# ScalarE and GpSimd in the order of the source in the recurrence and the attention of a hybrid decoder layer, and the work on loaded data issued later than the load

## The chip, the cores and the metric

The kernel runs on one core of one Trainium2 chip. Its engines are TensorE (PE in the profile: matmuls and transposes), VectorE (DVE), ScalarE (ACT), GpSimd (POOL) and the queue of SyncE (SP) that issues the DMAs. The metric is the device time of one launch in microseconds (us), lower is better.

## The reference

One decoder layer, 1024 tokens by 1024 features, all in float32:

```python
u = rmsnorm(x, mix_pre_norm)
z = u @ w_in                       # q,k,v of 3 groups x 4 heads; r,k,v and LoRA inputs of 8 RWKV heads; gates
# (A) dilated sliding-window attention, (window, dilation) = (128,1), (512,4), (2048,16)
q, k = rope(q), rope(k)
s = where(valid, q . k[t - dil*j] / 8, -inf);  o_g = softmax(s) @ v;  lse_g = m + log(den)
o_attn = sum_g softmax_g(lse)[g] * o_g
# (B) RWKV-7, per head, state 64 x 64, over the 1024 tokens
z = z + (token_shift(z) - z) * mu
decay = exp(-exp(-softplus(-(w0 + tanh(xw) @ w2)) - 0.5));  a = sigmoid(a0 + xa @ a2);  g = sigmoid(xg) @ g2
state = state * w_t + (state @ a_t) b_t^T + v_t k_t^T;  y_t = state @ r_t
o_rwkv = (groupnorm(y) * ln_w + ln_b + sum(r*k*r_k) * v) * g
# merge, MLP, per-layer embedding
h = x + rmsnorm((gate_a * (o_attn @ w_attn_up) + gate_b * (o_rwkv @ w_rwkv_up)) @ w_out)
h = h + rmsnorm(square(relu(rmsnorm(h) @ w_ff_in)) @ w_ff_out)
h = h + rmsnorm((p @ w_ple) * sigmoid(h @ w_ple_gate))
```

## The kernel before

**Arithmetic.** A float32 product is made of three passes: each operand is split into a high part (`uh`, `wh`) and a low part (`ul`, `wl`), and `mm3` sums high x high, high x low and low x high into one PSUM bank. So a weight tile of 128 x 1024 that SP has loaded as `wr` (`wload`) is split before it is used: ACT copies it to `wh`, POOL subtracts for `wl`. The pool of these three names has two buffers each. A dense body is a projection of one such tile with all tokens in two halves `z` of 512, with an evacuation behind each half (`add_z`, `zhalf`).

**Stages.** Norm and transposition of the input (0 to 44 us of the profiled span); recurrence (to about 540) in four pairs of heads w = 0 to 3, worked in 16 chunks of 64 tokens as a chain of small matmuls: `elementwise` (decay `En`, `Ep`, key `kk`, `BK`), `invert` and `fold` (the matrices `TM`, `AR` of a chunk), `scan` (over the chunks: PE's `q`, then DVE adds into `AR`), `read_out` (`y`), `post` (the group norm: ACT evacuates `y` to `yc`, squares it, PE sums (`hv`), ACT takes the root `vc`, spreads it to `rb`, PE transposes it (`yt`), three DVE operations on `yc`, and SP stores `oscr<-yc`; there is one `yc` tile, and `post` runs twice per pair, b = 0 and 1). Then the attention (to about 815) in six units n = 0 to 5 (three groups, two pairs of heads each): scores `sc`, masked by DVE into `SB`, exponent on ACT, transposes `pt`, DVE copies them to `PB`, and `po` is the product with the values. `q` and `k` of a unit are evacuated by `qk`: two ACT copies into the tile `qk`, four DMAs that exchange its halves into `sw`, DVE's product with the cosines in place (`qk<-qk,rope`), POOL's product of `sw` with the sines, DVE's sum. `combine` joins the groups (to 832); then merge, out projection, MLP (1040 to 1690) and the embedding.

**What sets the order.** PE's instructions stand in the order of the source for the whole kernel. That order is made by a planner at build time, `Order` (`sch`): chains are generators that say when they can go on by the planner's own clock (`sch.t`), and while none is due, `fill` issues the next matmuls of a dense body. `Engine` (V, S, G) adds up planned costs of DVE, ACT and POOL, `Loads` a planned 2.5 us (`HOP_DMA`) for each DMA. DVE stands in the order of the source only from the start of the recurrence to the start of `attention` (`in_turn`). Everything else, ACT, POOL and SP throughout and DVE in the other stages, is ordered by the framework's scheduler, which places an instruction by its own estimate of when its inputs are there.

All DVE, ACT and POOL operations are issued by one helper, line L108, and all DMAs by L121; PE's lines are `mm` L244, `tr` L252, and `mm3` L261, L263, L265. In after.py they are L115, L128, L267, L275 and L284, L286, L288.

Of the kernel before, what the change touches and what calls it, by code (L numbers as in the profile page):

```python
# [57 lines left out]

class Written:
# [17 lines left out]
class Engine:  # L77
# [3 lines left out]
    def __init__(self, eng, order, fixed, per):  # L81
        self.eng, self.order, self.fixed, self.per = eng, order, fixed, per
        self.end, self.table = 0.0, None
        self.spare = None

    def __getattr__(self, name):
        f = getattr(self.eng, name)

        def call(*a, **kw):
            n = max(math.prod(x.shape[1:]) for x in a if hasattr(x, "shape"))  # L90
            o = self.order
            us = self.fixed + n * self.per * (1.8 if name == "transpose" else 1.0)
            if name == "activation" and a[2] in TABLE and self.table != TABLE[a[2]]:
                us += 1.3
                self.table = TABLE[a[2]]
            ins = [x for x in (*a[1:], *kw.values()) if hasattr(x, "shape")]
            ready = max((o.written.since(x, self) for x in ins), default=0.0)
            while self.spare and self.end + SPARE < ready:
                spare, self.spare = self.spare, None
                dep, t = o.dep, o.t  # L100
                self.spare = spare if next(spare, None) else None
                o.dep, o.t = dep, t
            self.end = max(self.end, o.t, ready) + us
            for x in (a[0], kw.get("accum_out")):
                if x is not None:
                    o.written.put(x, self.end, self)
            o.dep = max(self.end, o.dep)
            return f(*a, **kw)  # L108
        return call
# [14 lines left out]
class Order:  # L124
# [4 lines left out]
    def __init__(self):  # L129
        self.t = self.dep = 0.0  # L130
        self.chains = []
        self.dense = []
# [20 lines left out]

    def pick(self):
# [10 lines left out]
    def fill(self):  # L165
        if self.cur is None:
            self.cur, self.nxt = self.nxt or self.pick(), None
            if self.cur is None:
                return False
            if not self.cur[1]:  # L170
                self.ahead()
# [43 lines left out]
def layer(ctx: ExitStack, tc: tile.TileContext, x, pT, wz, wup, w_out, wff1, w_ff2, w_ple, w_pleg,  # L215
# [5 lines left out]
    V = Engine(nc.vector, sch, 0.18, 0.00104)  # L221
# [60 lines left out]
    def wload(src, n=1024):  # L282
# [3 lines left out]
        S.activation(hi[:, :n], raw[:, :n], AF.Copy)  # L286
        lo = wpool.tile([128, 1024], F32R, name="wl")
        G.tensor_tensor(lo[:, :n], raw[:, :n], hi[:, :n], OP.subtract)  # L288
# [260 lines left out]
    def elementwise(w):  # L549
# [7 lines left out]
        yield from wait(lambda: "r" in RKV[w] and "k" in RKV[w])  # L557
# [232 lines left out]
    def read_out(w):  # L790
        d = U[w]
        AR, TM, UV = d["AR"], d["TM"], d["UV"]
        for b in range(2):
# [12 lines left out]
            sch.busy[tag] = sch.dep + 1.5  # L806
# [3 lines left out]
    def post(w, b, ps, tag):  # L810
        pc = lambda c: pr[:, c + w:c + w + 1]
        ts = halves[b]
        og = rtile([128, 512], "og", "pg")
# [51 lines left out]
    A = {}  # L865
# [8 lines left out]
    def add_attn(n):  # L874
# [10 lines left out]

        def qk(x):
            def evac(h, ps):
# [7 lines left out]
                if h == 1:  # L895
# [4 lines left out]
                    G.tensor_tensor(sw, sw, rope_t[g][:, 1], OP.mult)  # L900
                    V.tensor_tensor(z, z, sw, OP.add)
                    A[n]["qk"] = sch.dep
# [14 lines left out]
    def attention():  # L917
        yield from wait(lambda: ("P", NU - 1, 1) in done)
        in_turn.__exit__(None, None, None)
# [28 lines left out]
        for n in range(6):  # L948
# [6 lines left out]
            yield sch.until(A[n]["qk"])  # L955
# [8 lines left out]
        yield from combine(OT, OTB[:, 1], stat)  # L964
# [103 lines left out]
    def combine(OT, OA, stat):  # L1068
        sraw = rtile([128, 768], "sraw", "v")
        SY.dma_start(sraw, cst[:, C_SEL:C_SEL + 768])  # L1070
        sel = rtile([128, 6, 128], "sel", "px", F32R)
        V.tensor_copy(sel.rearrange("p a b -> p (a b)"), sraw)
# [32 lines left out]
        for b in range(2):  # L1105
# [18 lines left out]
            OA_t.append(sch.dep)  # L1124

# [3 lines left out]
    in_turn = tc.manual_schedule(engines={mybir.EngineType.DVE})  # L1129
# [32 lines left out]
    def load_or(w, eng):  # L1162
# [3 lines left out]
        S.activation(hl[:, 0], raw, AF.Copy)  # L1166
        eng.tensor_tensor(hl[:, 1], raw, hl[:, 0], OP.subtract)
        orT[w] = (hl[:, 0], hl[:, 1])

    def merge(j):  # L1170
        def load():
# [6 lines left out]
            for n in range(2):  # L1178
                SY.dma_start(gt[n], g_scr[2 * j + n])
                S.activation(gt[n], gt[n], AF.Sigmoid)  # L1180
# [537 lines left out]
```

## Time and profile before

| | |
|---|---|
| median of 3 runs | 1836.97 us (1831.67 to 1838.75) |
| profiled execution | 1831.63 us, span 1829.7 us |
| mean granted PE clock | 0.984 |
| busy: PE, DVE, ACT, POOL | 97%, 57%, 40%, 42% of the span |

The rows of the profile name the engine, the line, the operation and out<-in by the names of tiles. "[3.77 <-ACT wh]" behind a row is the time that the engine stood idle before it, and the instruction that ended that; in the table of waits the three numbers are microseconds in all, how often, and the longest. A matmul's own end is modelled, so PE's idle time is read from the waits and not from the gaps between rows.

### The profile page before, as it was taken

To read this page: it belongs to the slowest core of one execution; us is meant where nothing else is said; L and a number is where in the kernel's file an instruction comes from. 1 tells how busy PE (TensorE), PEld (TensorE's weight loads), DVE (VectorE), ACT (ScalarE), POOL (GpSimd) and SP (SyncE) were. 2 spreads that over 40 slices of the span, in tenths; PEclk is the share of its full clock that TensorE was granted. 3 is DMA by queue.
4 is the path that set the end of the run, shared out by engine and by line. 5 is a ranking of instruction groups with operands and counts; after the bars stand their busy time and mean duration, and the time that the engine had idled before them with its cause. 6 is when DMAs were issued, how large, how long until landed. Compare 5 with 4: busy or idle time off the path is not lost.

```text
span 1829.7 us, 25894 instructions
## 1 busy us (share of the span) xinstructions
PE 1769.9 (97%) x10192; PEld 1436.4 (79%) x10192; DVE 1044.6 (57%) x1866; ACT 725.5 (40%) x1300; POOL 775.1 (42%) x507
## 2 busy tenths in 40 slices
PE   9998989999989999999999999999999999999898
PEld 8887767777877777777888788888888888887787
DVE  6377686787332333352653655555555677888454
ACT  5934243322234443442443533333333333334354
POOL 1433132211133333322240166666666798896411
PEclk9998999899899999999999999999999999999999
DMA  4621121122232222232552311111121111112321
GB/s 158 221 87 42 53 93 36 49 68 104 70 109 81 58 58 59 83 128 107 182 166 78 119 58 47 58 47 56 41 77 46 47 47 50 55 47 82 103 80 47
DMA packets 51546, 146.13 MB, mean 80 GB/s; under 512 B 6241, under 2 KB 6625, under 8 KB 51426
## 3 DMA queue, kind: packets, MB, share of 16 engines
q1 hardware_dynamic: 51426, 144.49, 24.1%
q8 instruction: 80, 1.31, 0.3%
q14 instruction: 40, 0.33, 0.1%
HBM read 110.52 MB, written 27.26 MB: 75 GB/s over the span
## 4 chain that ended last, share of the span: by engine, by line
PE 67%; DVE 2%; ACT 1%; DMA 1%; POOL 0%; issue 0%; SPq 0%; DVEq 0%; ACTq 0%; POOLq 0%
PE z L263 14%; PE z L261 14%; PE z L265 14%; PE bk L261 7%; PE bk L263 7%; PE bk L265 7%; PE po L244 1%; PE sc L244 1%; PE pt L252 1%; DVE tot L108 1%; PE tp L252 1%; PE av L252 0%; DMA wr<-in_w_pleg_dram 0%; DVE yc L108 0%; DVE nm L108 0%
## 5 line engine op out<-in xcount | busy, mean ns | idle before, releaser
L108 POOL TENSOR_TENSOR wl<-wr,wh 128x1024 fp32r<-128x1024 f32 (+1 forms) x88 | 214.4, 2436 | 481.1 <-ACT wh L108 424.8
L108 DVE TENSOR_TENSOR tot<-tot,bk 128x512 f32<-128x512 f32 x468 | 308.0, 684 | 188.5 <-PE bk L265 187.8
L263 PE MATMUL z<-ul,wh 128*128 128x512 f32 (+1 forms) x800 | 320.0, 400 | 0.3 <-DVE ul L108 0.3
L261 PE MATMUL z<-uh,wh 128*128 128x512 f32 (+1 forms) x800 | 318.6, 398 | 0.9 <-ACT uh L108 0.9
L265 PE MATMUL z<-uh,wl 128*128 128x512 f32 (+1 forms) x800 | 316.4, 396 | 0.2 <-POOL wl L108 0.2
L261 PE MATMUL z<-f,wh 128*128 128x512 f32 x512 | 200.0, 391 | 1.9 <-ACT f L108 1.9
L263 PE MATMUL z<-f,wh 128*128 128x512 f32 x512 | 200.0, 391 | 0.2 <-DVE f L108 0.2
L265 PE MATMUL z<-f,wl 128*128 128x512 f32 x512 | 199.8, 390 | 0.0
L108 ACT ACTIVATE duo<-sum 128x512 fp32r<-128x512 f32 x150 | 90.3, 625 | 226.2 <-PE bk L265 120.9
L263 PEld LDWEIGHTS z<-ul,wh 128*128 128x128 f32 x800 | 153.1, 191 | 34.0 <-issue 8.1
L261 PEld LDWEIGHTS z<-uh,wh 128*128 128x128 f32 x800 | 153.1, 191 | 32.9 <-issue 5.6
L108 ACT ACTIVATE wh<-wr 128x1024 fp32r<-128x1024 f32 (+1 forms) x88 | 91.6, 1041 | 219.6 <-PE z L263 189.3
L265 PEld LDWEIGHTS z<-uh,wl 128*128 128x128 f32 x800 | 153.4, 192 | 28.5 <-issue 2.8
L261 PE MATMUL bk<-duo 128*128 128x512 f32 x420 | 163.4, 389 | 0.0
L263 PE MATMUL bk<-duo 128*128 128x512 f32 x420 | 163.4, 389 | 0.0
L265 PE MATMUL bk<-duo 128*128 128x512 f32 x420 | 163.4, 389 | 0.0
L108 POOL TENSOR_TENSOR duo<-sum,duo 128x512 fp32r<-128x512 f32 x75 | 101.0, 1347 | 102.3 <-ACT duo L108 102.3
L261 PEld LDWEIGHTS z<-f,wh 128*128 128x128 f32 x512 | 96.4, 188 | 22.2 <-ACT f L108 2.1
L263 PEld LDWEIGHTS z<-f,wh 128*128 128x128 f32 x512 | 96.5, 189 | 20.6 <-DVE f L108 0.5
L265 PEld LDWEIGHTS z<-f,wl 128*128 128x128 f32 x512 | 96.5, 189 | 20.0
L108 POOL TENSOR_TENSOR sum<-w2r 128x512 f32<-128x512 f32 x75 | 98.8, 1317 | 6.7 <-DVE yc L108 2.0
L108 POOL TENSOR_TENSOR sum<-hr 128x512 f32<-128x512 f32 x75 | 97.6, 1311 | 4.8 <-DVE duo L108 3.1
(302 smaller groups left out, 3196.8 us busy)
## 6 DMA issues: line engine op xcount, KB each, us to landing
wr<-in_wz_dram SPq DMA_DIRECT2D x48, 512.0 KB, 3.7
w2r<-in_w_ff_dram SPq DMA_DIRECT2D x32, 512.0 KB, 3.6
wr<-in_wff_dram SPq DMA_DIRECT2D x32, 512.0 KB, 3.5
xt<-in_x_dram SPq DMA_DIRECT2D x16, 512.0 KB, 4.3
gscr<-gst SPq DMA_DIRECT2D x32, 256.0 KB, 2.0
g<-gscr SPq DMA_DIRECT2D x16, 512.0 KB, 4.2
sw<-qk SPq DMA_DIRECT2D x48, 128.0 KB, 2.3
sascr<-lst SPq DMA_DIRECT2D x16, 256.0 KB, 4.2
```

What stands on the lines that cost most here:

```text
L108: return f(*a, **kw)
L244: PE.matmul(out_, a, b, start=start, stop=stop)
L252: PE.transpose(out_, a, ident if idn is None else idn)
L261: PE.matmul(ps, ah, bh, start=i == 0, stop=False)
L263: PE.matmul(ps, ah, bl, start=False, stop=False)
L265: PE.matmul(ps, al, bh, start=False, stop=i == n - 1)
```

## The change

- `in_turn`, the stretch in which instructions keep the order of the source, now covers DVE, ACT and POOL, and it lasts to the end of `combine`.
- `Order.soon(us, job)`: a job is issued `us` later on the planner's clock, at the latest when the next dense body begins. The split of a weight tile (`wload`), of a tile of the recurrence's output (`load_or`), and the sigmoids of the gates (`merge`) are such jobs, 3.9 to 4.5 us behind their load.
- `qk`: POOL's product and DVE's sum move into a chain `turned`, 2.7 us behind the DMAs. DVE's first product stays in the evacuation.
- `elementwise` waits until 2.7 us behind its loads; `post` waits for the post before it, and the bank of `y` is held until it is evacuated.
- The planned cost of a DVE operation with two inputs outside PSUM is 1.25 times what it was.
- The load of `sraw` moves ahead of unit 5, the copy `sel` ahead of `combine`.

```diff
@@ -56,6 +56,10 @@
     return x.tensor.name, (p, p + n, f, f + 1 + sum((k - 1) * s for s, k in free))
 
 
+def in_psum(x):
+    return "PSUM" in type(x.tensor if hasattr(x, "tensor") else x[:].tensor).__name__.upper()
+
+
 class Written:
 
 
@@ -78,8 +82,8 @@
 
 
 
-    def __init__(self, eng, order, fixed, per):
-        self.eng, self.order, self.fixed, self.per = eng, order, fixed, per
+    def __init__(self, eng, order, fixed, per, shared=False):
+        self.eng, self.order, self.fixed, self.per, self.shared = eng, order, fixed, per, shared
         self.end, self.table = 0.0, None
         self.spare = None
 
@@ -90,6 +94,9 @@
             n = max(math.prod(x.shape[1:]) for x in a if hasattr(x, "shape"))
             o = self.order
             us = self.fixed + n * self.per * (1.8 if name == "transpose" else 1.0)
+            if self.shared and sum(hasattr(x, "shape") and math.prod(x.shape[1:]) > 1 and not in_psum(x)
+                                   for x in (*a[1:], *kw.values())) > 1:
+                us *= 1.25
             if name == "activation" and a[2] in TABLE and self.table != TABLE[a[2]]:
                 us += 1.3
                 self.table = TABLE[a[2]]
@@ -129,6 +136,7 @@
     def __init__(self):
         self.t = self.dep = 0.0
         self.chains = []
+        self.jobs = []
         self.dense = []
         self.cur = self.nxt = None
         self.busy = {}
@@ -151,6 +159,17 @@
     def add(self, body, load=None, gate=None, late=False):
         self.dense.append((gate, load, body, late))
 
+    def soon(self, us, job):
+
+        jobs = [job]
+
+        def due():
+            yield us
+            if jobs:
+                jobs.pop()()
+        self.jobs.append(jobs)
+        self.spawn(due(), 0)
+
     def pick(self):
         for i, (gate, load, body, late) in enumerate(self.dense):
             if gate() if gate else i == 0:
@@ -167,6 +186,10 @@
             self.cur, self.nxt = self.nxt or self.pick(), None
             if self.cur is None:
                 return False
+            while self.jobs:
+                jobs = self.jobs.pop(0)
+                if jobs:
+                    jobs.pop()()
             if not self.cur[1]:
                 self.ahead()
         try:
@@ -218,7 +241,7 @@
     PE = nc.tensor
     sch = Order()
     SY = Loads(nc.sync, sch)
-    V = Engine(nc.vector, sch, 0.18, 0.00104)
+    V = Engine(nc.vector, sch, 0.18, 0.00104, True)
     S = Engine(nc.scalar, sch, 0.16, 0.00092)
     G = Engine(nc.gpsimd, sch, 0.15, 0.0022)
 
@@ -283,9 +306,15 @@
         raw = wpool.tile([128, 1024], F32, name="wr")
         SY.dma_start(raw[:, :n], src)
         hi = wpool.tile([128, 1024], F32R, name="wh")
-        S.activation(hi[:, :n], raw[:, :n], AF.Copy)
         lo = wpool.tile([128, 1024], F32R, name="wl")
-        G.tensor_tensor(lo[:, :n], raw[:, :n], hi[:, :n], OP.subtract)
+
+        def split():
+            S.activation(hi[:, :n], raw[:, :n], AF.Copy)
+            G.tensor_tensor(lo[:, :n], raw[:, :n], hi[:, :n], OP.subtract)
+        if ("X", 0) in done:
+            sch.soon(HOP_DMA + 1.4, split)
+        else:
+            split()
         return hi, lo
 
     def rstd_of(ss, name):
@@ -554,7 +583,8 @@
         a = rtile([128, T], "a", "a")
         SY.dma_start(En, sa_scr[2 * w])
         SY.dma_start(a, sa_scr[2 * w + 1])
-        yield from wait(lambda: "r" in RKV[w] and "k" in RKV[w])
+        t0 = sch.t + HOP_DMA + 0.2
+        yield from wait(lambda: sch.t >= t0 and "r" in RKV[w] and "k" in RKV[w])
         r, k = RKV[w]["r"], RKV[w]["k"]
         BK = rtile([128, NCH, 128], "BK", ("BK", "BK2")[w % 2])
         kk = rtile([128, T], "kk", "kk")
@@ -803,13 +833,14 @@
                     c = 8 * b + i
                     if c:
                         mm(ps[hp, i, :], AR[hp, 0, c - 1], AR[hp, 1, c], 0.06, start=False, stop=i == 7)
-            sch.busy[tag] = sch.dep + 1.5
+            sch.busy[tag] = 1e9
             sch.spawn(post(w, b, ps, tag), 2, 0.3)
         done.add(("S", w))
 
     def post(w, b, ps, tag):
         pc = lambda c: pr[:, c + w:c + w + 1]
         ts = halves[b]
+        yield from wait(lambda: (w, b) == (0, 0) or ("P", w - 1 + b, 1 - b) in done)
         og = rtile([128, 512], "og", "pg")
         bv = rtile([128, 512], "bv", "py")
         SY.dma_start(og, og_scr[w][:, ts])
@@ -883,6 +914,12 @@
             S.activation(dst.rearrange("p (r i) -> p i r", r=d)[:, h * (L // 2):(h + 1) * (L // 2), :],
                          ps.rearrange("p (i r) -> p i r", r=d), AF.Copy)
 
+        def turned(z, sw):
+            G.tensor_tensor(sw, sw, rope_t[g][:, 1], OP.mult)
+            yield sch.until(G.end)
+            V.tensor_tensor(z, z, sw, OP.add)
+            A[n].setdefault("qk", []).append(V.end)
+
         def qk(x):
             def evac(h, ps):
                 if h == 0:
@@ -897,9 +934,7 @@
                     for b in range(4):
                         SY.dma_start(sw[32 * b:32 * b + 32], z[32 * (b ^ 1):32 * (b ^ 1) + 32])
                     V.tensor_tensor(z, z, rope_t[g][:, 0], OP.mult)
-                    G.tensor_tensor(sw, sw, rope_t[g][:, 1], OP.mult)
-                    V.tensor_tensor(z, z, sw, OP.add)
-                    A[n]["qk"] = sch.dep
+                    sch.spawn(turned(z, sw), 1, HOP_DMA + 0.2)
             return evac
 
         def v_evac(h, ps):
@@ -916,7 +951,6 @@
 
     def attention():
         yield from wait(lambda: ("P", NU - 1, 1) in done)
-        in_turn.__exit__(None, None, None)
         amask = rtile([128, 384], "amask", "ex")
         SY.dma_start(amask, cst[:, C_BAND:C_BAND + 384])
         st = rtile([128, 512], "ast", "py")
@@ -952,7 +986,11 @@
             yield from wait(lambda: ("vk", n) in done)
             if n < 5:
                 sch.spawn(turn(n + 1), 2)
-            yield sch.until(A[n]["qk"])
+            yield from wait(lambda: len(A[n].get("qk", ())) == 2)
+            yield sch.until(max(A[n]["qk"]))
+            if n == 5:
+                sraw = rtile([128, 768], "sraw", "v")
+                SY.dma_start(sraw, cst[:, C_SEL:C_SEL + 768])
             yield from unit(n, g, hp, OT[g][:, hp], vkb[:, n % 2], SB, PB, amask)
             if n > 3:
                 load_or(5 - n, G)
@@ -961,7 +999,9 @@
                 load_or(3, V)
             if hp:
                 NAT[g] = yield from natural(g, stat)
-        yield from combine(OT, OTB[:, 1], stat)
+        sel = rtile([128, 6, 128], "sel", "px", F32R)
+        V.tensor_copy(sel.rearrange("p a b -> p (a b)"), sraw)
+        yield from combine(OT, OTB[:, 1], stat, sel)
 
     def unit(n, g, hp, o, vk, SB, PB, amask):
         d = DILS[g]
@@ -1065,11 +1105,7 @@
 
     oaT, OA_t = [], []
 
-    def combine(OT, OA, stat):
-        sraw = rtile([128, 768], "sraw", "v")
-        SY.dma_start(sraw, cst[:, C_SEL:C_SEL + 768])
-        sel = rtile([128, 6, 128], "sel", "px", F32R)
-        V.tensor_copy(sel.rearrange("p a b -> p (a b)"), sraw)
+    def combine(OT, OA, stat, sel):
         row = rtile([64, T], "row2", "v", F32R)
         V.memset(row.bitcast(F32), 0.0)
         M, den, t2 = stat(), stat(), stat()
@@ -1122,11 +1158,14 @@
                 V.tensor_tensor(lo[:, hs], o, hi[:, hs], OP.subtract)
             done.add(("A", b))
             OA_t.append(sch.dep)
+        in_turn.__exit__(None, None, None)
+        V.shared = False
 
     done.add(("X", 0))
     sch.t = V.end = S.end = G.end = 0.0
     sch.written = Written()
-    in_turn = tc.manual_schedule(engines={mybir.EngineType.DVE})
+    in_turn = tc.manual_schedule(
+        engines={mybir.EngineType.DVE, mybir.EngineType.Activation, mybir.EngineType.Pool})
     in_turn.__enter__()
     sch.spawn(lora_out(), 2)
     sch.spawn(rwkv(), 0)
@@ -1163,8 +1202,11 @@
         raw = wpool.tile([128, 1024], F32, name="wr")
         SY.dma_start(raw, o_scr[w])
         hl = rtile([128, 2, T], "orw", ("AR0", "AR1", "BK", "UV")[w], F32R)
-        S.activation(hl[:, 0], raw, AF.Copy)
-        eng.tensor_tensor(hl[:, 1], raw, hl[:, 0], OP.subtract)
+
+        def split():
+            S.activation(hl[:, 0], raw, AF.Copy)
+            eng.tensor_tensor(hl[:, 1], raw, hl[:, 0], OP.subtract)
+        sch.soon(HOP_DMA + 1.4, split)
         orT[w] = (hl[:, 0], hl[:, 1])
 
     def merge(j):
@@ -1177,7 +1219,11 @@
                 gt = [gt2[:, 0], gt2[:, 1]]
             for n in range(2):
                 SY.dma_start(gt[n], g_scr[2 * j + n])
-                S.activation(gt[n], gt[n], AF.Sigmoid)
+
+            def gates():
+                for g in gt:
+                    S.activation(g, g, AF.Sigmoid)
+            sch.soon(HOP_DMA + 2.0, gates)
             return hi, lo, gt
 
         def body(hi, lo, gt):
```

On ACT at the start of the recurrence, where the LoRA inputs `xw`, `xa`, `xg` are evacuated, put through their functions (with a table load each) and split (`xwh`, `xgr`), and `wh` is the high part of the first projections' weights. Before:

```order
L108 ACTIVATE xg<-z,omu 128x512
L108 ACTIVATE wh<-wr 128x1024
L108 ACTIVATE xw<-z,omu 128x512
L108 ACT_TABLE_LOAD
L108 ACTIVATE xw<-xw 96x1024
L108 ACTIVATE xg<-z,omu 128x512
L108 ACTIVATE xwh<-xw 96x1024
L108 ACTIVATE wh<-wr 128x1024
L108 ACT_TABLE_LOAD
L108 ACTIVATE xg<-xg 96x1024
L108 ACTIVATE r<-z,omu 128x512
```

and after:

```order
L115 ACTIVATE xg<-z,omu 128x512
L115 ACTIVATE xw<-z,omu 128x512
L115 ACT_TABLE_LOAD
L115 ACTIVATE xw<-xw 96x1024
L115 ACTIVATE xg<-z,omu 128x512
L115 ACTIVATE xwh<-xw 96x1024
L115 ACT_TABLE_LOAD
L115 ACTIVATE xg<-xg 96x1024
L115 ACTIVATE xgr<-xg 96x1024
L115 ACTIVATE xa_596<-xar 96x1024
L115 ACTIVATE wh<-wr 128x1024 x2
L115 ACTIVATE r<-z,omu 128x512
```

The first two splits now stand together, behind all of the LoRA work and directly ahead of the first evacuation `r`; before, the first stood ahead of that work and the second in the middle of it.

On ACT at the second `post` of the first pair (w = 0, b = 1), in which `yc<-y` fills the tile anew. `TQ`, `TN` and `TM` evacuate steps of the next pair's matrices, `gst` a gate. Before:

```order
L108 ACTIVATE v<-z,omu 128x512
L108 ACTIVATE part<-z,pr 128x512
L108 ACTIVATE yc<-y 128x512
L108 ACTIVATE wh<-wr 128x1024
L108 ACTIVATE v<-z,omu 128x512
L108 ACTIVATE part<-z,pr 128x512
L108 ACTIVATE TQ<-tq 32x512 x2
L108 ACTIVATE TN<-tr 32x16x32 x2
L108 ACTIVATE TM<-bt 128x4x128 x2
```

and after:

```order
L115 ACTIVATE vc<-hv,cs 128x8
L115 ACTIVATE rb<-vc 128x512
L115 ACTIVATE TQ<-tq 32x512 x2
L115 ACTIVATE sq<-y 128x512
L115 ACTIVATE yc<-y 128x512
L115 ACTIVATE gst<-z 128x512
L115 ACTIVATE TN<-tr 32x16x32 x2
L115 ACTIVATE TM<-bt 128x4x128
```

Between the `rb` of the first post and the `yc` of the second only `TQ` and `sq` are left, and `gst` and `TN` stand behind that `yc`.

On DVE at the end of an attention unit, where `PB` are the last copies that the unit's `po` matmuls need and `qk<-qk,rope` belongs to the next unit's projections. Before:

```order
L108 COPY PB<-pt 128x2x128
L108 TENSOR_SCALAR nm<-ast 128x2
L108 COPY PB<-pt 128x512
L108 COPY PB<-pt 128x2x128
L108 COPY PB<-pt 128x512
L108 TENSOR_TENSOR qk<-qk,rope 128x1024
L108 TENSOR_TENSOR qk<-qk,sw 128x1024
```

and after:

```order
L115 TENSOR_SCALAR nm<-ast 128x2
L115 COPY PB<-pt 128x2x128
L115 COPY PB<-pt 128x512
L115 TENSOR_TENSOR qk<-qk,rope 128x1024
L115 COPY PB<-pt 128x2x128
L115 COPY PB<-pt 128x512
L115 TENSOR_TENSOR qk<-qk,sw 128x1024
```

The product now stands ahead of the unit's last two copies, which it followed before.

## The prediction

> **What bounds the kernel now.** I read the page's busy line first, then the table by stage, the waits of TensorE (PE) in the two stages that the change touches, and last the stretches at half clock.
>
> ```profile
> span 1829.7 us, 25894 instructions
> PE 1769.9 (97%) x10192; PEld 1436.4 (79%) x10192; DVE 1044.6 (57%) x1866; ACT 725.5 (40%) x1300; POOL 775.1 (42%) x507
> ```
> ```profile
> core 0: us, PE busy (x) PEld busy (x) DVE busy (x) ACT busy (x) POOL busy (x), PEclk, DMA share, GB/s
> 100.00:560.00 460.00, 428.79 (x3822) 346.61 (x3818) 301.98 (x592) 155.90 (x256) 107.73 (x75) 0.95 0.21 68
> 560.00:850.00 290.00, 285.56 (x1549) 214.71 (x1546) 102.23 (x305) 117.00 (x257) 92.54 (x36) 1.00 0.27 84
> 1250.00:1670.00 420.00, 420.00 (x1855) 347.77 (x1854) 292.46 (x420) 154.05 (x248) 320.39 (x223) 1.00 0.15 48
> ```
>
> PE is busy for 97% of the span, and its matmuls are the same in number after the change. So the time can only move by PE's idle time and by its clock. The MLP, 1250 to 1670, has no idle time at all; it gives the pitch of a dense matmul, 420.00/1855 = 0.226 us. The recurrence (100 to 560) leaves 460 − 428.79 = 31.2 us idle, the attention with the combine (560 to 850) 4.4: 35.6 us is all that a better order can win there, beside the clock. What PE waited for, from 30 to 850:
>
> ```profile
> PE hs L244 <- ACT kk L108: 7.0, 1, 7.0
> PE q L244 <- DVE AR L108: 5.8, 4, 2.3
> PE yt L252 <- ACT rb L108: 3.3, 2, 2.4
> PE av L252 <- ACT v L108: 2.9, 4, 0.8
> ...
> PE hs L244 <- PE z L261: 1.2, 2, 0.6
> ```
>
> The first row is a single wait: ACT held `En<-Ep` ahead of `kk`. The second is the chain of small DVE operations of the recurrence. The rest is 1 to 3 us each. Now the clock, in rows of the table by stage again (PEclk is the number behind POOL's count):
>
> ```profile
> 146.10:153.10 7.00, 6.96 (x24) 6.22 (x25) 6.68 (x11) 3.01 (x4) 4.01 (x2) 0.50 0.00 0
> 453.90:467.10 13.20, 13.20 (x120) 11.27 (x121) 5.35 (x4) 4.50 (x7) 2.24 (x1) 0.50 0.19 61
> 324.00:334.00 10.00, 9.90 (x33) 8.55 (x34) 5.47 (x10) 5.65 (x8) 2.55 (x1) 0.50 0.17 63
> 1682.30:1686.10 3.80, 0.02 (x2) 0.01 (x1) 3.80 (x5) 1.15 (x2) 2.90 (x3) 0.95 0.49 143
> 1686.10:1689.10 3.00, 3.00 (x7) 2.42 (x8) 1.84 (x5) 1.89 (x5) 2.17 (x3) 0.50 0.93 346
> ```
>
> At 0.50 half of a stretch is lost: 3.5 us right behind the 7.0 us wait, 5.0 and 6.6 in the two long ones. The last pair shows the pattern outside the change: PE stood still for 3.8 us, and the 3.0 us after it ran at 0.50.
>
> **What goes.** In the new order ACT's `kk` and `rb`, the `v` evacuations and the splits (`wh` on ACT, `wl` on POOL) stand where the planner wants them, and PE has more dense matmuls between the steps of a chain. I let all waits go but three: q's 5.8 (its DVE operations stay beside POOL's subtractions, below), 1.2 of hs behind z (PE behind itself), and 1.5 left over of the small ones. So 35.6 − 8.5 = 27.1 us go, least 15 (hs, rb, av and part of the rest), most 35.6. Of the clock goes the 3.5 us behind the hs wait and half of 5.0 + 6.6: 9.3, least 0, most 15.1. The planner's new costs of V, its waits on loads, `post` waiting for the post before and holding its `y` bank issue no new work and act through the order that is priced here: nothing by themselves. `sraw` and the `sel` copy come earlier in the attention, beside idle engines (DVE 102 us of 290): nothing, 1 us if they are late. The split of the gates' sigmoids in the merge lies behind the part in source order: nothing, within 2 us.
>
> **What comes: the start of the recurrence.** Before, ACT split the first weights (`wh<-wr`) ahead of the LoRA work; now both splits stand behind it. All of it is work that ACT did before, so its rows price it:
>
> ```profile
> 47.61 0.67 ACT L108 ACTIVATE xg<-z,omu 128x512 f32<-128x512 f32 x1
> 48.18 1.05 ACT L108 ACTIVATE xwh<-xw 96x1024 fp32r<-96x1024 f32 x1
> 49.13 1.04 ACT L108 ACTIVATE wh<-wr 128x1024 fp32r<-128x1024 f32 x1
> 50.19 1.28 ACT L108 ACT_TABLE_LOAD   x1
> 51.48 1.06 ACT L108 ACTIVATE xg<-xg 96x1024 f32<-96x1024 f32 x1
> ...
> 53.02 1.05 ACT L108 ACTIVATE xgr<-xg 96x1024 fp32r<-96x1024 f32 x1
> ...
> 54.53 1.05 ACT L108 ACTIVATE xa<-xar 96x1024 fp32r<-96x1024 f32 x1
> ```
> ```profile
> 43.80 0.40 PE L261 MATMUL z<-uh,wh 128*128 128x512 f32 x1
> ```
> ```profile
> 42.19 2.40 POOL L108 TENSOR_TENSOR wl<-wr,wh 128x1024 fp32r<-128x1024 f32 x1 [24.13 <-ACT wh L108]
> ```
> ```profile
> 42.72 1.88 DVE L108 SCALAR_TENSOR_TENSOR xw<-edges,pr,xw 128x1 f32<-128x1 f32 x1 [0.82 <-ACT xw L108]
> ```
>
> PE began the first body of the recurrence at 43.80, when the last LoRA projection was through. Now ACT does, from there, xg, xwh, the table load, xg, xgr, xa and only then wh, and PE stands for 0.67 + 1.05 + 1.28 + 1.06 + 1.05 + 1.05 + 1.04 = 7.2 us. SP's load of these weights moves behind the three `xar<-xw` DMAs, which are through by then. The third matmul of the body needs `wl` too, which takes POOL 2.40 more, while PE has two pitches of work (0.45): 2.0 us. I take 9.3; if ACT's overlaps of 0.1 count it is 8.8, if `xa` has to wait for those DMAs, 11.
>
> **What comes: the second post of a pair.** `post(w,1)` begins with ACT's `yc<-y`, and the store `oscr<-yc` of the first half still reads the tile that it writes. In the chain that ended last before:
>
> ```profile
> 523.52 0.76 DVE yc L108
> ...
> 526.18 3.59 DMA oscr<-yc
> ...
> 529.86 0.61 ACT yc L108
> ```
> ```profile
> DMA to landing us min/median/max: 2.0/3.4/5.4
> ```
>
> From the first half's first DVE step, three of these (523.52 to 525.8) and the store, ACT's `yc` came 529.86 − 523.52 = 6.3 us later. Before, other ACT work was placed ahead of it; now ACT holds there in source order. Behind it stand `gst` and `TN` (w=0), `wh`, `vc` and `rb` (w=1), `vc` and `rb` (w=2 and 3), and PE waits for each of these. PE has 1 to 3 us of dense work left in the meantime, so 6.3 less that: 5.5, 4.3, 3.0 and 3.7 at the four places, 16.5 in all. With a store of 2.0 instead of 3.6 it is 10, with 5.4, 24. That these sites hide it would need some 15 more dense matmuls in each.
>
> **What comes: the rotary step.** DVE writes `qk<-qk,rope` in place, so it waits for the four `sw<-qk` DMAs that read `qk`:
>
> ```profile
> L108 DVE TENSOR_TENSOR qk<-qk,rope 128x1024 f32<-128x1024 f32 x12 | 14.7, 1225 | 82.3 <-DMA sw<-qk 82.3
> L108 DVE COPY PB<-pt 128x512 f32<-128x512 f32 x22 | 15.0, 685 | 3.7 <-PE pt L252 3.6
> ```
> ```profile
> 624.59 1.22 DVE L108 TENSOR_TENSOR qk<-qk,rope 128x1024 f32<-128x1024 f32 x1 [6.93 <-DMA sw<-qk]
> ```
> ```profile
> 619.23 1.09 ACT L108 ACTIVATE qk<-z 128x512 f32<-128x512 f32 x1
> ```
> ```profile
> 620.35 2.42 SPq L121 DMA_DIRECT2D sw<-qk  x4
> ```
>
> From the issue to DVE's start are 624.59 − 620.35 = 4.2 us, and 82.3/12 = 6.9 is DVE's mean idle time before it: mostly harmless, as it stood between units. The new `turned` moves only POOL's product and DVE's sum behind the load; this first product stays at the evacuation, and now DVE has it ahead of work that PE waits for at 7 of 12 places. At an attention unit's end: evacuation 1.1, DMAs 4.2, product 1.2, `PB` 0.7, in all 7.2 us until PE can go on, against 12 to 15 dense matmuls that PE's new order has there, 2.7 to 3.4 us: some 4.2 at each of four sites (4.6, 4.3, 4.2, 3.9 by their counts), 1.5 at a fifth with more of them. Inside the recurrence it stands ahead of `TM<-fq` of the last fold (4.2 + 1.2 + 0.7, some 6) and of the `AR` of the last scan (4): 18.5 + 10 = 28.5. If half of the sites have other cover it is 14; with the mean of 6.9 it is 45.
>
> **What comes: the rest.** In the combine the third `load_or` has to wait for one of two `wr` buffers with ACT and DVE behind it: 2.5 us (0 to 5). Then the clock: about ten of these waits are longer than 2.5 us. The nearest rows are the 3.0 us at 0.50 behind a wait of 3.8, so 1.5 us lost, and the 3.5 lost behind 7.0. Some of the ten will bring none, so I take a little under the smaller, 1.2 each: 12 us (5 to 25).
>
> The Trainium skill (TensorE: Matmul & The Clock Gate, "What's actually happening") says that the clock halves after an idle window of about 3.4 us and is back after one busy window. By it only the waits above 3.4 us would count, eight of them at 1.7 us, an estimate of 14 us in place of my 12; the stretches of 10.0 and 13.2 us above are longer than one such window, and there the measurement decides.
>
> The row of the 128x1 operation, 1.88 us on one column, ends at 44.60, as POOL's `wl` (42.19 + 2.40) does: DVE stood until POOL was through. That is why I leave q's 5.8 us in, although the planner now adds 25% for such operations. The Trainium skill (SBUF — State Buffer, "SBUF: two separate sides") calls the pair of ports that the two engines share an exclusive lock held for the whole instruction; by it a 25% surcharge is too little where they meet and too much elsewhere, and the trace agrees with its 1.88 us.
>
> **The sum.** Gone: 27.1 + 9.3 = 36.4. New: 9.3 + 16.5 + 28.5 + 2.5 + 12 = 68.8. Net +32.4 on the profiled 1831.6 us (span 1829.7 and 1.9 around it), so 1864. This execution is at the low end of the three runs, 5.4 below their median of 1836.97; taking two thirds of that back, I forecast 1868, 31 above the median. About 0.5%, 9 us, is what can be told from no change.
>
> **Rivals.**
> 1. Faster. The new order hides its own waits: the planner's dense matmuls cover the rotary step and the second post (both priced by me from counts of matmuls behind them), and only the start is lost. Then 27.1 + 9.3 go and 9.3 + 3 come: 24 less than the median, about 1813. For it speaks that PE has more dense work between the steps; against it, that this work is 2.7 to 3.4 us where 7.2 are needed. It decides when the new waits with their clock come to less than 36 − 9 = 27 us. Chance 0.12.
> 2. No change: half the rotary sites and half the posts are hidden (14 + 8 + 9 + 5 = 36 against 36 gone): 1837, within 9. Chance 0.10.
> 3. Slower still: DVE's late work at one place makes the next evacuation late, so that PSUM banks are not free and each wait starts a half clock of 10 us as at 324 and 454. Ten waits at 5 us in place of 1.2 add 38: about 1906. Against it: the stretches behind a long wait were 3 and 7 us. Chance 0.08.
> My forecast, in-order waits of about 55 us of which half is paid for by those removed, has 0.70.
>
> The range: with the rotary step at 14 and posts at 10 the sum falls by 21, and if all 35.6 us of waits go by another 8.5: 1838, which I round to 1836. With posts at 24 and rotary at 38 it rises by 17, with clock 20 by 8: 1893. I take 1836 to 1894. Faster 0.12, same 0.11, slower 0.77.
>
> **What would show it.** In the trace after: PE idle for 8 to 11 us at 44 behind ACT `wh` and POOL `wl`; ACT `yc<-y` idle behind `oscr<-yc` four times with 3 us or more; PE waits `po` behind DVE `PB` near 4 us, several times, and DVE's idle time before `qk<-qk,rope` still near 80 us; hs behind `kk`, av behind `v` gone; window 560 to 850 some 20 us longer. I would be wrong if the rope's product came between units (then 1813 to 1840), or if PE's waits fell below 30 us in 30 to 850.

## The result: slower by 3%, and the profile after

The changed kernel takes 1890.9 us (median of 4 runs, 1888.8 to 1891.4) against 1837.0: ratio 1.030 with a 95% interval of 1.027 to 1.032. The profiled execution took 1891.4 us with a span of 1889.6, 59.9 longer than before. The same lines of its page:

```profile
span 1889.6 us, 25877 instructions
PE 1791.9 (95%) x10192; PEld 1448.6 (77%) x10192; DVE 1079.0 (57%) x1866; ACT 728.1 (39%) x1301; POOL 773.4 (41%) x507
```

PE has the same 10192 matmuls, so the page splits the loss by itself. PE's busy time grew by 22.0 us (1769.9 to 1791.9), which is clock; its idle time grew by 37.9 (59.8 to 97.7). What it waited for from 30 to 900 us, the rows over 1 us:

```profile
PE po L267 <- DVE PB L115: 25.3, 10, 6.1
PE z L288 <- POOL wl L115: 8.9, 4, 5.4
PE z L284 <- ACT wh L115: 8.1, 1, 8.1
PE q L267 <- DVE AR L115: 5.5, 3, 3.6
PE yt L275 <- ACT rb L115: 5.5, 3, 2.4
PE z L284 <- ACT part L115: 4.7, 2, 3.3
PE cb L267 <- DVE row L115: 3.3, 1, 3.3
PE bt L275 <- ACT TN L115: 3.2, 1, 3.2
PE A L267 <- DVE BK L115: 2.7, 1, 2.7
PE z L284 <- ACT gst L115: 2.1, 1, 2.1
PE tq L267 <- DVE TN L115: 1.3, 1, 1.3
```

Of the rows shown before, hs behind ACT's `kk` (7.0) and av behind `v` (2.9) are gone. In their place stand waits that were not there or were small: `po` behind `PB` ten times (before, 2.3 us in two), the projections `z` behind `wh` and `wl` (before, 0.2 us once), and behind the evacuations `part` and `gst` that free their banks.

The longest wait for `PB`, as DVE, POOL and PE show it (start, length, then the operation, and in brackets the idle time before it and what ended it):

```profile
604.73 0.75 DVE L115 COPY PB<-pt 128x256 f32<-128x256 f32 x2
611.07 3.41 DVE L115 TENSOR_TENSOR qk<-qk,rope 128x1024 f32<-128x1024 f32 x1 [5.59 <-DMA sw<-qk]
614.40 0.74 DVE L115 COPY PB<-pt 128x256 f32<-128x256 f32 x2
```
```profile
611.06 2.34 POOL L115 TENSOR_TENSOR sw<-sw,rope 128x1024 f32<-128x1024 f32 x1 [14.47 <-DMA sw<-qk]
```
```profile
614.87 0.69 PE L267 MATMUL po<-PB,vkb 128*64 128x128 f32 x4 [6.06 <-DVE PB L115]
```

DVE had nothing to do but the two copies, and stood 5.6 us for the exchange that its next instruction in order needs. That instruction then took 3.41 us. At all twelve products (q and k of six units) the same landing releases DVE's product and POOL's, and they start within 0.1 us of each other. At eleven of them DVE starts first and takes 1.23 us, and POOL's takes 3.4; here POOL's started first and took 2.34 us, and DVE's took the 3.41. PE stood 6.06 us in all. Over the twelve products DVE's idle time is 104.1 us:

```profile
L115 DVE TENSOR_TENSOR qk<-qk,rope 128x1024 f32<-128x1024 f32 x12 | 16.9, 1407 | 104.1 <-DMA sw<-qk 104.1
```

The second post of the first pair, on ACT:

```profile
286.84 0.60 ACT L115 ACTIVATE yc<-y 128x512 f32<-128x512 f32 x1 [4.36 <-DMA oscr<-yc]
287.33 0.59 ACT L115 ACTIVATE gst<-z 128x512 f32<-128x512 f32 x1
287.95 1.07 ACT L115 ACTIVATE TN<-tr 32x512 f32<-32x512 f32 x2
```

`TN` is what PE's 3.2 us wait (bt) was for. In the whole trace ACT stood four times and 17.2 us for that store, against 5.3 before.

One wait that the prediction did not have, on POOL and PE at the last unit:

```profile
846.46 3.40 POOL L115 TENSOR_TENSOR sw<-sw,rope 128x1024 f32<-128x1024 f32 x1 [7.14 <-PE z L288]
849.82 2.33 POOL L115 TENSOR_TENSOR wl<-wr,wh 128x1024 fp32r<-128x1024 f32 x1
```
```profile
852.21 0.79 PE L288 MATMUL z<-uh,wl 128*128 128x512 f32 x1 [5.41 <-POOL wl L115]
```

POOL, in source order too, held the product of the rotary step ahead of a weight tile's low part, and stood 7.14 us before it.

### The profile page after: what moved, and what is told of

Same layout as the page of the kernel before. It is cut to its first block, busy times and chain, and to the rows that moved or that the text cites. A ratio compares the mean times of both kernels' runs of the same rounds, so it can differ in the third digit from the quotient of the medians.

```text
span 1889.6 us, 25877 instructions
## 1 busy us (share of the span) xinstructions
PE 1791.9 (95%) x10192; PEld 1448.6 (77%) x10192; DVE 1079.0 (57%) x1866; ACT 728.1 (39%) x1301; POOL 773.4 (41%) x507
## 4 chain that ended last, share of the span: by engine, by line
PE 80%; DVE 9%; ACT 3%; issue 3%; DMA 2%; POOL 1%; SPq 1%; DVEq 0%; POOLq 0%; ACTq 0%
PE z L288 16%; PE z L284 16%; PE z L286 16%; PE bk L284 6%; PE bk L288 6%; PE bk L286 6%; DVE xy L115 1%; DVE pt L115 1%; DMA sw<-qk 1%; DVE tot L115 1%; DVE yc L115 1%; PE sc L267 1%; PE tp L275 1%; PE y L267 1%; SPq L128 1%
## 5 line engine op out<-in xcount | busy, mean ns | idle before, releaser
L284 PE MATMUL z<-uh,wh 128*128 128x512 f32 (+1 forms) x800 | 325.4, 407 | 15.5 <-ACT wh L115 8.1
L288 PE MATMUL z<-uh,wl 128*128 128x512 f32 (+1 forms) x800 | 325.2, 406 | 9.1 <-POOL wl L115 8.9
L286 PE MATMUL z<-ul,wh 128*128 128x512 f32 (+1 forms) x800 | 324.5, 406 | 0.3 <-DVE ul L115 0.3
L284 PEld LDWEIGHTS z<-uh,wh 128*128 128x128 f32 x800 | 156.3, 195 | 49.9 <-ACT wh L115 8.3
L115 ACT ACTIVATE wh<-wr 128x1024 fp32r<-128x1024 f32 (+1 forms) x88 | 91.1, 1036 | 59.9 <-PE z L286 51.7
L115 POOL TENSOR_TENSOR sw<-sw,rope 128x1024 f32<-128x1024 f32 x12 | 39.9, 3328 | 175.4 <-DMA sw<-qk 153.6
```

The source lines that it names most:

```text
L284: PE.matmul(ps, ah, bh, start=i == 0, stop=False)
L286: PE.matmul(ps, ah, bl, start=False, stop=False)
L288: PE.matmul(ps, al, bh, start=False, stop=i == n - 1)
```

## The experiments

Each run's ratio is to the kernel before, run on the same chip (medians 1833.7 for e1 to e4, 1836.2 for e5 to e8, 1834.9 for e9 to e12). A difference in us from the changed kernel, whose 1890.9 stands against 1837.0, runs across chips; where the ratios say something else, their figure stands beside it.

**e1, the rotary product behind its DMAs.**

```diff
         def turned(z, sw):
+            V.tensor_tensor(z, z, rope_t[g][:, 0], OP.mult)
             G.tensor_tensor(sw, sw, rope_t[g][:, 1], OP.mult)
...
-                    V.tensor_tensor(z, z, rope_t[g][:, 0], OP.mult)
-                    sch.spawn(turned(z, sw), 1, HOP_DMA + 0.2)
+                    sch.spawn(turned(z, sw), 1, HOP_DMA + 3.0)
```

> The changed kernel (1890.9 us), but DVE's product qk<-qk,rope is also issued in the chain that follows the exchange, and that chain starts 5.5 us behind the DMAs on the planner's clock in place of 2.7. Theory A (the engines held in source order by a wait are the price): the waits po<-PB (25.3 us, 10 times) and q<-AR's long one (3.6) go, and with them most of the half clock behind them (six windows of together 31 us, up to 15 us lost): 25 to 42 us less, 1849 to 1866. Rival B (the new order of PE and the planner's costs stretch the chains by themselves, and DVE's place does not matter): po waits for something else, less than 10 us gained.

Measured: 1847.7 us, ratio 1.008 (1.006 to 1.010), 43 less than the changed kernel (40 by the ratios). Theory A holds, with 1.3 us more than the far end of its range. Page and waits of its trace:

```profile
PE 1775.5 (96%) x10192; PEld 1439.0 (78%) x10192; DVE 1064.3 (58%) x1866; ACT 726.0 (39%) x1299; POOL 770.8 (42%) x507
```
```profile
PE po L267 <- DVE PB L115: 7.0, 7, 1.5
```

`po` fell from 25.3 to 7.0. Of the 44.2 us of span, 16.4 are PE's busy time, less half clock, and 27.8 are idle time. The run moves two things: DVE's product, and the start of the whole chain, with POOL's product in it, from 2.7 to 5.5 us behind the DMAs. So the waits for `wl` behind the start are gone too (8.9 to 1.6). In e6 below, where POOL's long waits go and DVE's product stays in the evacuation, `po` is still 21.1; so `po` goes with DVE's product, or with the later chain, and not with POOL's waits. How the 43 us divide between the two moves was not tried.

**e2, two buffers for `yc`.**

```diff
-    BUFS = {"gst": 2}
+    BUFS = {"gst": 2, "yc": 2}
```

> The changed kernel with two buffers for the tile yc (two padding tiles of 288 bytes are left out to make room), so that ACT's copy of the second post does not wait for the store of the first. Theory A: ACT's idle time of 17.2 us before yc goes, PE's bt<-TN (3.2) and yt<-rb (5.5) with it, and the half clock behind them (about 3 us lost): 8 to 13 us less, 1878 to 1883. Rival B: the posts' waits come from the small ACT operations of the post itself, which are as many as before: less than 4 us gained.

Measured: 1874.1 us (1870.2 to 1880.1), ratio 1.022 (1.020 to 1.025), 17 less (14 by the ratios). ACT's wait for the store is gone:

```profile
L115 ACT ACTIVATE yc<-y 128x512 f32<-128x512 f32 x8 | 4.7, 592 | 0.0
```

PE's waits for `bt` and `tq` are gone with it, and `yt` falls from 5.5 to 0.7; A behind `BK` grew from 2.7 to 5.2. The direction is theory A's; the gain is at the top of its 8 to 13 or above. The profiled execution was the slowest of the four, so its trace does not show where the last 4 us lie, and that stays open, as does any share that the left-out padding has.

**e3, the first split ahead of the LoRA work.**

```diff
+    for w in range(NU):
+        add_rkv(w)
+    sch.ahead()
     done.add(("X", 0))
...
-    for w in range(NU):
-        add_rkv(w)
```

> The changed kernel, but the first weight tile of the recurrence is loaded and split before the stretch in source order begins, so that its ACT copy stands ahead of the LoRA work, as in the kernel before. Theory A: the waits of 8.1 us for wh and 1.6 for wl at 45 us go, and most of the half clock of 10.2 us behind them (up to 5 lost): 11 to 15 us less, 1876 to 1880. Rival B: the LoRA chain on ACT is the bound there and PE waits for its results a little later: less than 5 us gained.

Measured: 1878.3 us, ratio 1.025 (1.023 to 1.027), 12.6 less, inside theory A's 11 to 15; by the ratios it is 9, a little below. Its trace has no wait over 1 us before 149 us, and the wait for `gst` that ends at 240.28 in the changed kernel ends 10.2 us earlier.

**e7, matmuls without use in the start's wait.**

```diff
+    keep = psum.tile([128, 512], F32, name="keep", tag="m0")
+    for i in range(32):
+        PE.matmul(keep, uT[0][0][:, 0, 0:128], uT[0][0][:, 0, :], start=True, stop=True)
```

> The changed kernel with 32 matmuls of 128x512 whose product is not read, in PE's order at the start of the recurrence, where PE stands for 8.1 us: PE has 7 us of work there, and nothing else moves. Theory A (the half clock of 10.2 us behind that wait is caused by the idle time): the window at 50 us runs at full clock, 3 to 5 us less than 1890.9, though PE's first body starts no earlier. Rival B (the half clock comes from what PE does or from the fp32 work behind it): no change, or longer by what the 32 matmuls overrun.

Measured: 1889.1 us, ratio 1.028 (1.026 to 1.031), 2 less than the changed kernel and inside its interval. What the experiment was for is seen in the stretch itself: the table by stage (PEclk is the number behind POOL's count) for the changed kernel and then for e7.

```profile
44.00:53.00 9.00, 0.86 (x9) 0.66 (x7) 3.98 (x5) 8.90 (x10) 0.00 (x0) 0.83 0.20 46
53.00:64.00 11.00, 9.40 (x29) 7.07 (x30) 0.55 (x1) 1.70 (x3) 5.07 (x2) 0.68 0.29 95
```
```profile
44.00:53.00 9.00, 8.14 (x40) 6.53 (x38) 3.96 (x5) 8.91 (x10) 0.00 (x0) 1.00 0.20 46
53.00:64.00 11.00, 8.91 (x31) 6.89 (x32) 0.57 (x1) 2.17 (x3) 5.07 (x2) 0.84 0.30 97
```

With PE kept busy the clock behind the wait was 0.84 and not 0.68: half of the loss in these 11 us went, and a wait of 2.1 us for `wl` that stayed still has its own. By the clock that the traces record it ran at 0.50 from 49.9 to 60.1 us in the changed kernel, from inside the wait on, and here from 57.0 to 60.4. So idle time starts the half clock, as theory A has it; its 3 to 5 us are not to be seen in the time of the whole.

**e4, DVE alone in source order.**

```diff
-    in_turn = tc.manual_schedule(
-        engines={mybir.EngineType.DVE, mybir.EngineType.Activation, mybir.EngineType.Pool})
+    in_turn = tc.manual_schedule(engines={mybir.EngineType.DVE})
```

> The changed kernel with DVE alone in source order (to the end of the combine); ACT and POOL are placed by the framework's scheduler as in the kernel before. Theory A: what ACT's and POOL's source order costs goes (start 9.7, posts about 9, waits on part and gst 6.8, combine and wl 10, and 12 of clock), what DVE's order costs stays (po, q): 30 to 45 us less, 1846 to 1861. Rival B: the scheduler's own misplacements return with it (hs<-kk was 7.0, av<-v 2.9, yt 6 us before) and outweigh it: less than 15 us gained, 1876 or more.

Measured: 1859.0 us, ratio 1.014 (1.012 to 1.016), 32 less (29 by the ratios). In time theory A holds, but rival B's waits are there too:

```profile
PE po L267 <- DVE PB L115: 19.5, 6, 6.0
PE hs L267 <- ACT kk L115: 14.4, 3, 6.1
```

So source order on ACT and POOL does what it was to do, it takes away 14.4 us of hs behind `kk`; it costs more at other places. `po` is DVE's and stays.

**e8, e1 and e4 together.**

> The edits of e1 and e4 together: the rotary product behind its DMAs, DVE alone in source order, ACT and POOL placed by the scheduler. Theory A: e4's 1859 less the 19.5 us of po, the long q of 4.2 and their half clock: 1820 to 1832, at or just below the kernel before (1833.7 on the chip of e1 to e4). Rival B: the scheduler's hs<-kk (14.4 us in e4) grows as DVE's operations change place: 1840 or more.

Measured: 1824.5 us, ratio 0.993 (0.991 to 0.995): below the kernel before, by 0.7%. Theory A holds. hs behind `kk` is 14.6 us in its trace, as in e4, so it did not grow.

**e5, the edits of e1, e2 and e3, and the source order ended at the start of the combine.**

```diff
     def combine(OT, OA, stat, sel):
+        in_turn.__exit__(None, None, None)
...
-        in_turn.__exit__(None, None, None)
```

> The changed kernel with the three edits of e1, e2 and e3 together, and the source order of DVE, ACT and POOL ends at the start of the combine in place of its end. Theory A (separate stalls at separate places): the three gains add (43 + 17 + 13 us) and the combine's waits (cb<-row 3.4, wl behind sw) go too: 1810 to 1818, below the kernel before. Rival B (the waits take each other's place, so that part of each gain is the same gain): 1825 to 1845.

Measured: 1818.4 us, ratio 0.989 (0.987 to 0.992), 72.5 less than the changed kernel; the three alone gave 43.2 + 16.8 + 12.6 = 72.6. That these agree so closely is partly chance: by the ratios e5 is 74 us less and the three together 62, and the difference of 12 is about as large as its own uncertainty. What the runs show is that none of the three gains is mostly the gain of another, as rival B would have it: the stalls are separate in the main. The fourth edit wasn't tried alone: the wait cb behind `row` is gone from the trace, but `po` has four of 1 to 2 us in the last unit. Its page and largest waits:

```profile
PE 1765.7 (97%) x10192; PEld 1432.0 (79%) x10192; DVE 1068.8 (59%) x1866; ACT 726.0 (40%) x1299; POOL 769.0 (42%) x507
```
```profile
PE po L266 <- DVE PB L115: 11.3, 10, 1.9
PE A L266 <- DVE BK L115: 5.2, 1, 5.2
PE z L283 <- ACT part L115: 3.3, 1, 3.3
```

**e6, the split at the load again.**

```diff
-        if ("X", 0) in done:
-            sch.soon(HOP_DMA + 1.4, split)
-        else:
-            split()
+        split()
```

> The changed kernel, but the split of a weight tile is issued at its load again, not 3.9 us later on the planner's clock (load_or and the gates stay as they are). Theory A (an instruction that waits holds its engine in source order): ACT stands about 2 to 3.5 us before each of 46 copies wh, 90 to 160 us in all, and PE gets a third of that: 25 to 70 us more than 1890.9, 1915 to 1960. Rival B: the load is issued a whole body (48 matmuls of 0.226 us, 11 us) ahead, and ACT has this time to spare: within 9 us of 1890.9.

Measured: 1867.6 us, ratio 1.017 (1.015 to 1.019): 23 less than the changed kernel. Both theories were wrong. A row of ACT, one of POOL and one of DVE show what differs (in the last column the idle time before), and one of PE what stays:

```profile
L115 ACT ACTIVATE wh<-wr 128x1024 fp32r<-128x1024 f32 x46 | 48.6, 1058 | 0.2 <-DMA wr<-in_wz_dram 0.2
```
```profile
L115 POOL TENSOR_TENSOR sw<-sw,rope 128x1024 f32<-128x1024 f32 x12 | 40.0, 3333 | 14.3 <-DMA sw<-qk 12.2 <-PE z L288 1.1 <-PE fq L267 1.0
```
```profile
L115 DVE TENSOR_TENSOR qk<-qk,sw 128x1024 f32<-128x1024 f32 x12 | 14.7, 1221 | 13.8 <-POOL sw L115 13.8
```
```profile
PE po L267 <- DVE PB L115: 21.1, 5, 6.1
```

The rows of POOL and DVE in the changed kernel:

```profile
L115 POOL TENSOR_TENSOR sw<-sw,rope 128x1024 f32<-128x1024 f32 x12 | 39.9, 3328 | 175.4 <-DMA sw<-qk 153.6 <-PE z L288 21.8
L115 DVE TENSOR_TENSOR qk<-qk,sw 128x1024 f32<-128x1024 f32 x12 | 31.6, 2634 | 13.7 <-POOL sw L115 13.7
```

ACT stood 0.2 us in all for 46 loads (0.0 in the changed kernel): the data was there when the split's turn came, so there was no wait for `soon` to take away. A likely reason, not tried, is that SP's queue is ordered by the scheduler, which can issue a load ahead of its place in the source. In the changed kernel POOL stood 153.6 us for `sw<-qk` ahead of other work, here 12.2, PE's 8.9 us of z behind `wl` are 1.6, and DVE's sums take 14.7 us in place of 31.6. Of the 18.9 us of span in its profile, 9.3 are PE's busy time.

**e9, e5 without the later split.**

> The kernel of e5 (1818 us) with the split of a weight tile at its load again, as in e6. Theory C (in the changed kernel the later split cost 23 us only because it put POOL's wl and sw and DVE's rotary step behind one another, and e5 has moved these apart): within 9 us of e5, 1809 to 1827. Rival D (a later split makes wh and wl late for PE wherever it stands): 12 to 23 us less, 1795 to 1806.

Measured: 1808.0 us (1807.9 to 1814.0), ratio 0.986 (0.983 to 0.989), 10 below e5 (6 by the ratios). It lies between the two theories' ranges, a microsecond below theory C's, and its interval overlaps e5's, so how much of the 23 us came from that meeting of POOL and DVE stays open. It has the lowest median here, ahead of both kernels, with e11 below within its interval:

```profile
PE 1762.4 (98%) x10192; PEld 1431.2 (79%) x10192; DVE 1056.2 (58%) x1866; ACT 723.7 (40%) x1299; POOL 768.8 (43%) x507
```
```profile
PE z L283 <- ACT part L115: 5.8, 1, 5.8
PE po L266 <- DVE PB L115: 4.1, 3, 1.9
```

**e10, e5 without the 25% on DVE's planned cost.**

> The kernel of e5 without the 25% on the planned cost of DVE operations with two inputs outside PSUM. Theory C (the planner's cost moves a few dense matmuls and no wait): within 9 us of e5, 1809 to 1827. Rival D (the 25% gives the chains the room that they need beside POOL): q<-AR and A<-BK waits grow by 6 us or more with their half clock, 1828 or more.

Measured: 1827.9 us, ratio 0.996 (0.994 to 0.997), 9.4 above e5 (12 by the ratios), at the edge between the two theories' ranges. So the 25% is worth something, but not where rival D had it: q is 2.5 us and the waits of A are small, and two others appear, for the matmuls `bc` of the key's norm:

```profile
PE bc L274 <- DVE yc L115: 6.5, 1, 6.5
...
PE bc L274 <- ACT kk L115: 5.0, 1, 5.0
```

**e11, e5 with POOL placed by the scheduler.**

> The kernel of e5 with DVE and ACT in source order, POOL placed by the framework's scheduler. Theory C (once its own wait on the exchange is moved, POOL's order costs and gains nothing): within 9 us of e5, 1809 to 1827. Rival D (POOL's place decides which DVE operation it meets): more than 9 us either way, seen in q<-AR and A<-BK (7 us together in e5).

Measured: 1810.9 us, ratio 0.987 (0.984 to 0.989), 7.6 below e5 (5 by the ratios) with overlapping intervals: inside theory C's range. POOL's source order gained nothing here.

**e12, e5 with DVE alone in source order.**

> The kernel of e5 with DVE alone in source order; ACT and POOL are placed by the scheduler. Theory C (source order of ACT wins as much, hs<-kk 14.6 and tq 4.3 in e8, as it loses, and its losses are now mended): e8's waits return and their half clock with them, 1822 to 1832, above e5. Rival D (source order of ACT and POOL is worth nothing by itself): within 5 us of e5's 1818 or below it.

Measured: 1822.9 us, ratio 0.993 (0.991 to 0.996): theory C's range, with hs behind `kk` back at 14.2 us. Against e5 (0.989) it is 4.5 us more (7 by the ratios) and the intervals overlap. Its nearest neighbour is e11, on the same chip, which differs from it in ACT alone: with ACT in source order too the time is 12.0 us less, the two intervals (0.984 to 0.989 and 0.991 to 0.996) are apart, and there is no wait of hs behind `kk`. Of the 10.7 us by which the spans of the two profiles differ, 8.1 are PE's busy time. So with its own stalls mended, source order on ACT is worth some 12 us; on POOL (e5 against e11) no gain was seen. What DVE's source order is worth in the attention was not tried: every run here keeps it.

## Why the prediction was right, and which terms were not

The forecast was 1868 in a range of 1836 to 1894, slower; 1890.9 is inside, near the top. Point by point:

- **The waits that go.** hs behind `kk`, av and the old yt waits went. q, which I left standing at 5.8, fell to 1.9: its 5.5 after has the 3.6 of the rotary step in it. e11 and e12 show that ACT's order is what takes hs away.
- **The start.** 9.3 us forecast; 8.1 for `wh` and 1.6 for `wl` measured, and e3 takes them away with the clock behind them: 9 to 13 us.
- **The second post.** The wait is where it was put, four times, but mis-sized: I had 16.5 us for PE, and bt and yt are 8.7 (3.2, 2.4, 1.25 and 1.9 at the four places). From DVE's first step to ACT's `yc` it was 5.0 us and not 6.3, as the stores landed in 2.0 to 3.0 us and not 3.6; the rest of the difference is that PE had more work left. With the half clock e2 puts its worth at 14 to 17.
- **The rotary step.** 28.5 us forecast; `po` is 25.3 and the long q wait 3.6, together 28.9. That the totals agree is luck: I had 18.5 for `po`, which is 6.8 more, and 10 for the two places inside the recurrence, which cost 0.9 (`kx` behind `TM`) and 3.6. One row differs in kind: `po` was five long waits of 3 to 6 us and five short ones, and POOL's product starting first (3.41 in place of 1.23 us) made the worst one longer. e1 took most of it away.
- **The combine.** `cb<-row` is 3.3 us against 2.5.
- **Not foreseen.** `wl` beyond the start (7.3 of the 8.9 us; the 5.4 shown are POOL's `sw` ahead of it, where the rest comes from stays open), `part` (4.7) and `gst` (2.1): 14 us. The first I should have had from POOL's order, where the moved product stands ahead of the split; I followed only DVE and ACT there.
- **The clock.** This is the term that failed in size. I had 12 us of new half clock and 9.3 of old gone, net 2.7; PE's busy time says 22.0. I counted ten waits above 2.5 us at 1.2 us each, and both figures were too small. By the clock that the traces record, the changed kernel has 15 stretches at 0.50 between 30 and 930 us, where the kernel before has 5. PE worked 76 us in them against 38, so it lost 19 us more there. Each of the 20 stretches lasted 3.4, 6.8, 10.2 or 13.7 us, so one that PE works through costs at least 1.7 us; the row of 3.0 us that I priced from is PE's part of one of 3.4. And 2.5 us is no bound for the wait. In the kernel before, these two stretches without work lie directly ahead of the 10.0 and the 13.2 us at 0.50 in the prediction (just before the second PE ran 32 matmuls of 32x32):

```profile
321.70:324.00 2.30, 0.05 (x1) 0.05 (x1) 2.27 (x4) 0.46 (x1) 1.80 (x3) 0.96 0.32 75
451.80:453.90 2.10, 0.03 (x1) 0.03 (x2) 0.80 (x2) 1.19 (x2) 0.00 (x0) 0.91 0.03 11
```

The changed kernel shows the same:

```profile
238.10:240.30 2.20, 0.05 (x2) 0.02 (x1) 1.09 (x3) 2.17 (x4) 1.57 (x1) 1.00 0.00 0
241.10:244.40 3.30, 3.30 (x9) 2.62 (x8) 0.96 (x4) 0.56 (x1) 2.59 (x1) 0.50 0.40 156
364.10:366.50 2.40, 0.04 (x1) 0.00 (x0) 0.87 (x2) 2.13 (x5) 0.98 (x1) 1.00 0.17 61
367.40:370.70 3.30, 3.30 (x10) 2.53 (x9) 3.16 (x5) 0.25 (x1) 1.84 (x3) 0.50 0.42 129
499.60:500.90 1.30, 0.00 (x0) 0.00 (x0) 1.27 (x2) 0.00 (x0) 0.00 (x0) 1.00 0.00 0
503.90:514.10 10.20, 10.20 (x89) 8.64 (x88) 0.85 (x1) 2.97 (x5) 0.00 (x0) 0.50 0.01 2
```

Waits of 2.2 and 2.4 us were each followed, within 1 us, by 3.3 us at 0.50. After 499.6 PE stood for 1.3 us only, then ran 64 matmuls of 32x32 in 2.2 us, and 10.2 us at 0.50 began 0.8 us behind them. The Trainium skill (TensorE: Matmul & The Clock Gate, "What's actually happening") has the clock halve after an idle window of about 3.4 us; as a bound for a single wait this trace does not agree, with its 2.2 us.

The three rivals: the first (faster, the dense matmuls cover the waits) is excluded by e1 to e3; the second (no change) by the time; of the third, the longer half clocks came in part (15 stretches at a mean of 5.7 us, not 10), and so did late evacuations (`part` and `gst`, 6.8 us).

Idle and clock together: +37.9 and +22.0 make the 59.9 us of span. By the sum it was +29.7 and +2.7. That the time is inside the range all the same owes something to luck: the clock came out 19 us above its term and 14 us of waits were not foreseen, while the posts came out 7.8 us and q 3.9 us below theirs.

## What to carry to other kernels

An engine that is put into source order stands at every instruction whose inputs are late, and what counts is who waits for the instructions behind it: look in the new order for each operation that a DMA releases, reads that must end before a tile is written again included, and move it behind the landing or give it a second buffer. Done here at three places, and with the source order ended before the combine, the same change went from 3.0% slower to 1.1% faster, and to 1.4% without the delayed splits. With the three places mended, source order on ACT was itself worth some 12 us. Price a stall of PE with its clock: of the 44 us of span that e1 took away more than a third was half clock, and here waits of 2.2 us already went with it.

## What the runs showed of the hardware

- PE's clock fell to half behind single waits of 2.2 to 2.4 us, and for 10.2 us behind a wait of 1.3 us followed by small matmuls. Each of the 20 stretches at half clock between 30 and 930 us in the traces before and after lasted 3.4 us or two, three or four times that. Matmuls without use in a wait of 8 us raised the next 11 us from 0.68 to 0.84.
- A DVE product of 128x1024 and a POOL product of the same size that one landing released ran one behind the other at all twelve places: the first took its 1.23 us (DVE, eleven times) or 2.34 us (POOL, once), the other some 3.4.
- With 46 splits issued directly at their loads, and the loads' queue ordered by the scheduler, ACT stood for 0.2 us in all (e6).
